# Projection by 512 tokens for eleven column groups, gelu and forget columns copied by ScalarE, row maxima paced by due steps, first attention operands loaded during the projection

## The chip, the cores and the metric

The kernel runs on one core of one Trainium2 chip. A core has TensorE (PE in the profile; PEld is its weight load), VectorE (DVE), ScalarE (ACT), GpSimd (POOL) and SyncE (SP), which here issues every DMA. The metric is the device time of one execution in microseconds; a comparison takes the median of several runs of each kernel.

## What is computed

One layer of a decoder trunk over 4096 tokens of width 1024, all in float32. The input is normed and projected to 3848 columns; three mixers read them, and their 1024 output columns are projected back, added to the input and normed.

```
h = rmsnorm(x, norm_g);  proj = h @ w_in          # (4096, 1024) @ (1024, 3848)
a_u a_v a_z | b_q b_fl b_i b_z | c_q c_k c_v c_z c_fl = split(proj)   # 256 each, c_*: 512, c_fl: 8
y_a = gelu(a_u) * (tril(w_s) @ layernorm(gelu(a_v)) + b_s) * silu(a_z)   # per 128-token chunk and group of 64
y_b = hgrn2(b_q, b_fl, b_i) * silu(b_z)           # gated linear recurrence, chunks of 128, 4 heads
y_c = softmax(c_q c_k^T / 8 + cumulative log-forget, causal) c_v * silu(c_z)   # 8 heads of 64
out = rmsnorm(x + [y_a | y_b | y_c] @ w_out, final_norm_g)
```

## The kernel before

Products of float32 matrices are split: an operand is held as a high part (type fp32r) and the rest (low part), and a product is the sum of high x high, high x low and low x high. So a projection over 1024 input rows is a chain of 8 x 3 = 24 matmuls into one PSUM buffer.

**Projection phase** (L177 to L1088). The tokens form 16 tiles of 256 (T), in 4 blocks of BT = 4. The loop at L1037 takes for each block the 15 column groups in the list `order` (b_fl, b_q, b_i, c_k, c_q, c_v, c_z, a_v, a_u, a_z, b_z; the last block has its own order, with c_v at the end), and for each group the four tiles: 60 steps to a block, 240 in all. A step calls `project` (L891): two halves, each of 24 matmuls with a moving operand of 256 columns, into one buffer acc of 2 x 256. In feature-major groups (c_q, c_k, c_z, b_fl, b_q; L902) the weights are stationary and 256 tokens move; in the others (L923) 128 tokens are stationary and 256 weight columns move, so the output has tokens on the partitions. b_i also carries the 8 forget columns of C (264 columns). There are two acc buffers (psa), so a step waits until the result of the step before the last has been copied out by `evac` (L841).

The order on TensorE is the program's order, written out by hand (manual_schedule); the other engines' order and the buffers of each pool are set by a scheduler. Between steps the loop advances a set of generators by one yield each, so that their TensorE work stands between projections: `xprep` (L256: load, norm, transpose the input of a tile, split it into hhi and hlo, in hT), `hgrn` (L413: the recurrence of one tile, 7 levels that each take a decay tile e from POOL, L493 and L494), `gm_v`, `gm_u`, `gm_z` (L753 to L814, the gMLP branch, whose gelu at L741 first copies acc with VectorE, L744), `hg_z`, `cgen` (the cumulated log-forget), and in the last block `prerm` (L948), the row maxima of the first U0 = 3 attention units. y_a and y_b are made with tokens on the partitions and turned by four transposes in `y_store` (L791, L797). Weights for the next group are loaded in a group's first step and split in the next two (L227, L228). Four tiles of hT exist; tile T is given up after its step of the last group, b_z (L1054), and the next block's input takes its place.

**Attention phase** (from L1092). A unit u = (p, Q) is a pair of heads p (4) with 512 queries Q (8): 32 units. Unit u goes over groups j = 0..Q of 512 keys, 144 groups in all; a group has 8 score tiles (`do_tile`, L1372: two matmuls, L1380 and L1383, then the exponential on ScalarE, L1387), indexed n = 0..7, two to a step si. The weighted values (`do_pv`, L1280) of a group are taken in the next group at n = 2, and `do_accs` (L1263) sums the probabilities on VectorE and POOL. When a unit is done, `finish_unit` sums its denominators (pl, L1223) and divides.

The softmax needs each row's maximum before the scores. A generator `rowmax` (L1145) makes them ahead: a step of it is two products (L127) into a buffer sm of which there are two, reduced by VectorE (L140, or L135 on the diagonal); after a unit's last product `rm_tail` (L1173) waits 6 yields, transposes the maxima through the same two buffers (mt, L1181) and copies them (L1183). Pacing: a step at n = 0, 1, 4, 6 of each group always, and at n = 3, 5, 7 while the count of maxima is below 2 * si + LEAD, LEAD = 8 * NJ + 12 = 76. A unit takes 8 * (Q + 1) maxima. Ahead of each unit's load, steps are forced until its maxima are there (L1429). Keys come into 26 buffers (big); a list `need` with due steps orders their loads, and unit 0's qa and qc are loaded at the start of the phase (L1361).

**Output phase** (from L1442): for each 128 tokens two chains of 24 matmuls with 512 columns (L1481), the residual and the final norm.

Of the kernel before, what the change touches and what calls it, by code (L numbers as in the profile page):

```python
# [33 lines left out]
def tile_trunk(  # L34
# [27 lines left out]
    const = ctx.enter_context(tc.tile_pool(name="const", bufs=1))  # L62
    dram = ctx.enter_context(tc.tile_pool(name="dram", bufs=1, space=DRAM))
# [46 lines left out]
    def load_keys(t, p, j):  # L110

        nc.sync.dma_start(t[0:64].bitcast(F32), prow(d_kh[j], p))
        nc.sync.dma_start(t[64:68].bitcast(F32), d_cb[j][2 * p : 2 * p + 2].rearrange("h r t -> r h t"))

# [62 lines left out]
    with ExitStack() as p1:  # L177
        cst = p1.enter_context(tc.tile_pool(name="cst", bufs=1))
        hp = p1.enter_context(tc.tile_pool(name="hp", bufs=BT))
        wp = p1.enter_context(tc.tile_pool(name="wp", bufs=2))  # L180
        xp = p1.enter_context(tc.tile_pool(name="xp", bufs=4))
# [60 lines left out]
        def x_ssq(t, ss):  # L242
            junk = wk.tile([P, D], BF16, tag="junk", name="junk")
            nc.scalar.activation(junk, t, AF.Square, accum_out=ss)
# [11 lines left out]
        def xprep(T, own_norm=False):  # L256

            xts = [x_load(2 * T + half) for half in range(2)]
# [14 lines left out]
            while len(hT) >= BT:  # L273
                yield
            hi = hp.tile([P, KC, 256], F32R, tag="hhi", name="hhi")
            lo = hp.tile([P, KC, 256], F32R, tag="hlo", name="hlo")
            hT[T] = (hi, lo)
            for half in range(2):
# [8 lines left out]
                for kk in range(2):  # L287
                    dst = (slice(None), slice(4 * kk, 4 * kk + 4), slice(half * P, half * P + P))
# [12 lines left out]
        def setup_gen():  # L301

            setup["lng"] = row_bcast("lng", ln_g.rearrange("o g c -> o (g c)"), 256)
            off = setup["off"] = row_bcast("lnb", ln_b.rearrange("o g c -> o (g c)"), 256)
# [8 lines left out]
            ws = wk.tile([P, 4, P], F32, tag="e", name="ws", bufs=3)  # L313
# [18 lines left out]
            nc.tensor.transpose(pt2[:, 4:6], lbr, ident[:2, :2])  # L332
            nc.vector.tensor_copy(bsT, pt2[:, 0:4])

# [24 lines left out]
            nc.vector.tensor_tensor(off4, off4, bcast(bsT[:, :, None], [P, 4, 64]), op=ALU.add)  # L359

# [7 lines left out]
            for li, h in enumerate(levels[2:]):  # L368
                nblk = 64 // h
                mt = wk.tile([P, 64], F32, tag="e", name="mt", bufs=3)  # L370
# [12 lines left out]
                m16 = wk.tile([P, 16], F32, tag="e", name="m16", bufs=3)  # L383
# [29 lines left out]
        def hgrn(T):  # L413
# [5 lines left out]
            l = wk.tile([P, 512], F32, tag="e", name="l", bufs=3)  # L419
# [20 lines left out]
            qk = wk.tile([P, 512], F32, tag="e", name="qk", bufs=3)  # L440
# [5 lines left out]
            for st in range(len(levels) + 4):  # L446
# [1096 lines left out]
```

## Time and profile before

| what | us |
|---|---|
| runs: median of three (lowest to highest) | 3445.62 (3445.28 to 3450.19) |
| profiled execution | 3452.37 |
| its span, first to last instruction | 3450.7 |
| TensorE busy in the span | 3316.0 |
| VectorE busy | 2367.5 |
| ScalarE busy | 1614.1 |
| GpSimd busy | 1428.7 |

The profile is of one execution; its span starts with the first instruction. A row of the costliest groups names line, engine, operation, output and inputs, shape and count, then the busy time of the group, the mean ns of one, and the idle time of the engine just ahead of them with what ended it. Weight loads, matmuls and DMAs have rows of their own. fp32 matmuls that are not split appear as two records each.

### The profile page before, as it was taken

The page shows a single profiled execution, that of the slowest core. Times are in us where ns is not written, and L with a number is a line of the kernel's source. Part 1 is how long each engine was busy: PE and PEld are TensorE (multiplying, and loading weights), DVE is VectorE, ACT ScalarE, POOL GpSimd, SP SyncE. Part 2 cuts the span into 40 slices and gives each one's busy share as a digit, 9 for nine tenths or more (in the row PEclk, how much of TensorE's full clock was granted, in tenths as well). Part 3 has the DMA queues.
Part 4 walks back from the last instruction along what each step waited for, and adds up shares of the span by engine and source line. Part 5 has one row for each costly group of instructions (what it writes and reads, how often), then busy time and mean ns, then how long its engine had stood idle before and what let it go on. Part 6 is the DMA issues. An engine that isn't in the chain of part 4 may idle for free.

```text
span 3450.7 us, 62925 instructions
## 1 busy us (share of the span) xinstructions
PE 3316.0 (96%) x24375; PEld 2634.7 (76%) x24375; DVE 2367.5 (69%) x4551; ACT 1614.1 (47%) x2947; POOL 1428.7 (41%) x1504
## 2 busy tenths in 40 slices
PE   7999999999999999989899999999999999999998
PEld 7999999999999999889555555555555555548887
DVE  6467745586457855695488788888888888755554
ACT  6335553356434453354255455555555555552221
POOL 2134422243224431343266566666666666660000
PEclk9999999999999999999799999999999999999999
DMA  5332243214232133211641142014201311014442
GB/s 181 112 96 66 77 138 118 84 53 156 90 109 75 41 112 115 73 53 56 156 113 27 30 120 67 24 34 124 66 24 34 108 50 42 28 65 147 144 144 98
DMA packets 227596, 297.70 MB, mean 86 GB/s; under 512 B 19602, under 2 KB 172448, under 8 KB 227298
## 3 DMA queue, kind: packets, MB, share of 16 engines
q1 hardware_dynamic: 227298, 293.69, 28.1%
q8 instruction: 191, 3.13, 0.4%
q14 instruction: 107, 0.88, 0.1%
HBM read 208.96 MB, written 84.43 MB: 85 GB/s over the span
## 4 chain that ended last, share of the span: by engine, by line
PE 72%; DVE 18%; ACT 3%; DMA 2%; POOL 2%; issue 2%; SPq 0%; DVEq 0%; POOLq 0%; ACTq 0%
PE acc L902 16%; PE pv L1280 12%; PE acc L923 11%; PE o L1481 10%; PE st L1380 7%; PE sm L127 6%; PE st L1383 6%; DVE mp L140 3%; DVE acc L1263 3%; DVE wlo L228 2%; DMA x<-in_x_dram 2%; PE pl L1223 1%; DVE gt L746 1%; DVE xq L511 1%; PE plb L574 1%
## 5 line engine op out<-in xcount | busy, mean ns | idle before, releaser
L1387 ACT ACTIVATE pt<-st,bias 128x512 f32<-128x512 f32 (+3 forms) x1152 | 700.4, 651 | 499.0 <-PE st L1383 466.9
L1263 POOL TENSOR_TENSOR acc<-acc,pt 128x512 f32<-128x512 f32 (+2 forms) x516 | 639.0, 1238 | 303.1 <-PE st L1380 221.3
L140 DVE TENSOR_REDUCE mp<-sm 128x2 f32<-128x1024 f32 (+1 forms) x460 | 535.4, 1191 | 163.6 <-PE sm L127 163.1
L902 PE MATMUL acc<-hhi,whi 128*128 128x256 f32 x2048 | 580.0, 288 | 4.2 <-DVE q L735 2.6
L902 PE MATMUL acc<-hhi,wlo 128*128 128x256 f32 x2048 | 568.0, 282 | 0.0
L902 PE MATMUL acc<-hlo,whi 128*128 128x256 f32 x2048 | 567.4, 281 | 0.1
L923 PE MATMUL acc<-whi,hhi 128*128 128x256 f32 (+1 forms) x1792 | 518.0, 289 | 18.5 <-DVE gu L744 16.1
L923 PE MATMUL acc<-wlo,hhi 128*128 128x256 f32 (+1 forms) x1792 | 507.0, 283 | 0.0
L923 PE MATMUL acc<-whi,hlo 128*128 128x256 f32 (+1 forms) x1792 | 506.8, 283 | 0.0
L1280 PE MATMUL pv<-pt,v 128*64 128x512 f32 (+3 forms) x2304 | 503.7, 578 | 0.8 <-POOL pt L1392 0.6
L1380 PE MATMUL st<-qa,ka 128*128 128x512 f32 (+2 forms) x1152 | 466.9, 407 | 18.0 <-DMA ka<-d_kl 12.5
L1263 DVE TENSOR_TENSOR acc<-acc,pt 128x512 f32<-128x512 f32 (+2 forms) x516 | 414.4, 803 | 91.7 <-PE pv L1280 51.7
L1383 PE MATMUL st<-qc,kb 68*128 68x512 f32 (+2 forms) x1152 | 442.9, 385 | 1.4 <-DMA qc<-mr 0.8
L127 PE MATMUL sm<-kb,qb 66*128 66x512 f32 (+2 forms) x1152 | 359.2, 394 | 33.2 <-DVE mp L140 26.0
L902 PEld LDWEIGHTS acc<-hhi,whi 128*128 128x128 f32 x2048 | 384.5, 190 | 7.9 <-DVE q L735 3.0
L902 PEld LDWEIGHTS acc<-hhi,wlo 128*128 128x128 f32 x2048 | 384.4, 190 | 0.0
L902 PEld LDWEIGHTS acc<-hlo,whi 128*128 128x128 f32 x2048 | 383.9, 189 | 0.5 <-DVE hlo L290 0.3
L1280 PEld LDWEIGHTS pv<-pt,v 128*64 128x64 f32 x2304 | 158.0, 140 | 286.5 <-issue 265.0
L1380 PEld LDWEIGHTS st<-qa,ka 128*128 128x128 f32 x1152 | 220.7, 192 | 185.8 <-issue 126.1
L923 PEld LDWEIGHTS acc<-whi,hhi 128*128 128x128 f32 x1792 | 341.8, 191 | 22.3 <-DVE gu L744 16.6
L923 PEld LDWEIGHTS acc<-wlo,hhi 128*128 128x128 f32 x1792 | 342.1, 191 | 0.1
L923 PEld LDWEIGHTS acc<-whi,hlo 128*128 128x128 f32 x1792 | 341.5, 191 | 0.0
(265 smaller groups left out, 5131.9 us busy)
## 6 DMA issues: line engine op xcount, KB each, us to landing
wraw<-in_w_in_dram SPq DMA_DIRECT2D x120, 512.0 KB
x<-in_x_dram SPq DMA_DIRECT2D x88, 512.0 KB
qa<-d_qh SPq DMA_DIRECT2D x64, 256.0 KB
out_dram<-x SPq DMA_DIRECT2D x31, 512.0 KB
kb<-d_kh SPq DMA_DIRECT2D x38, 256.0 KB
d_kh<-chi SPq DMA_DIRECT2D x32, 256.0 KB
d_kl<-clo SPq DMA_DIRECT2D x32, 256.0 KB
d_qh<-chi SPq DMA_DIRECT2D x32, 256.0 KB
```

Source lines behind the costliest of these rows:

```text
L127: nc.tensor.matmul(ps[:, :n], qb[0:66, h, i * P : (i + 1) * P], kb[0:66, h, :n], start=True, stop=True)
L140: nc.vector.tensor_reduce(dst, ps, axis=AX.X, op=ALU.max)
L228: nc.vector.scalar_tensor_tensor(lo[:, k, :n], raw, g, hi[:, k, :n].bitcast(F32), op0=ALU.mult, op1=ALU.subtract)
L511: nc.vector.tensor_tensor(xq[rows, :, r, :].rearrange("p g (n h) -> p g n h", h=h), sl(e), sl(qf), op=ALU.mult,)
L902: nc.tensor.matmul(ps[:, a, :], ww[:, k, cs], hh[:, k, :], start=n == 0, stop=n == 3 * KC - 1)
L923: nc.tensor.matmul(o, hh[:, k, ts_], ww[:, k, :width], start=n == 0, stop=n == 3 * KC - 1)
L1263: ins = eng.tensor_tensor(a[:, q0:], src[:, q0:], pts[i][:, q0:], op=ALU.add)
L1280: mm = nc.tensor.matmul(pv[64 * h : 64 * h + 64, q0:], vt[:, i, 64 * h : 64 * h + 64], group[h][i][:, q0:], start=kb == 0, stop=kb == nkb - 1,
L1380: first = nc.tensor.matmul(st[:, qm:], ka_t[g][:, h, cs], qa_t[u % 2][:, h, qm:], start=True, stop=False)
L1383: nc.tensor.matmul(st[:, qm:], kb_t[g][0:68, h, cs], qc_t[u % 2][:, h, qm:], start=False, stop=True)
L1387: nc.scalar.activation(pt[:, q0:], st[:, q0:], AF.Exp, bias=bias_of[u][:, h, kb : kb + 1])
L1481: nc.tensor.matmul(ps, a[:, k % 4, o : o + P], b[k][:, cs], start=n == 0, stop=n == 3 * KC - 1)
```

## The change

- Hidden tiles hold 512 tokens (J = T // 2), two of them in place of four; a pair is given up after two steps of b_z. Eleven groups (b_fl after the first block's, b_q, c_k, c_q, c_z, and now also a_u, a_z, b_z) are projected with 128 stationary weight columns and 512 moving tokens (`project_fm`); a step is one half a of the columns for 512 tokens instead of both halves for 256. Only b_i, c_v0, c_v1 and a_v keep tokens on the partitions.
- The gMLP branch and the gate of B work with features on the partitions: the mixing product is transposed, its affine part is one fused VectorE operation for each half, y_a needs no transposes, and y_b's gate is applied as the transposed tile is read.
- gelu's first copy goes from VectorE to ScalarE; the forget columns are copied by ScalarE, and GpSimd adds their bias.
- Buffers: xp is kept for all phases; tag e has 2 in place of 3, st 4 in place of 5, f and q 3 of double size in place of 5 and 4; the attention's big has 24 in place of 26.
- `prerm` may start from the third group of the last block; after it, `preload` loads unit 0's qa, qc, ka and kb into the xp buffers.
- Row maxima: steps at n = 3, 5, 7 are taken while the count is below `rm_due`; the tail waits 5 yields and is advanced right after a product instead of ahead of the next; no step at n = 0, 1 of the first group. A unit's closing work is advanced at n = 5, 6, 7 in place of 4, 5, 7. LEAD, which now only orders key loads, is 88.

```diff
-        hp = p1.enter_context(tc.tile_pool(name="hp", bufs=BT))
+        hp = p1.enter_context(tc.tile_pool(name="hp", bufs=BT // 2))
...
-            while len(hT) >= BT:
+            while J not in hT and len(hT) >= BT // 2:
                 yield
-            hi = hp.tile([P, KC, 256], F32R, tag="hhi", name="hhi")
-            lo = hp.tile([P, KC, 256], F32R, tag="hlo", name="hlo")
-            hT[T] = (hi, lo)
+            if J not in hT:
+                hT[J] = tuple(hp.tile([P, KC, 512], F32R, tag=f"h{c}", name=f"h{c}") for c in ("hi", "lo"))
+            hi, lo = hT[J]
...
-                    e = wk.tile([P, 512], F32, tag="e", name="e", bufs=3)
+                    e = wk.tile([P, 512], F32, tag="e", name="e", bufs=2)
...
-            nc.vector.tensor_copy(dst, ps)
+            nc.scalar.copy(dst, ps)
             nc.scalar.activation(t, dst, AF.Square)
...
+            pm = pst.tile([P, 2, 256], F32, tag="tp", name="pm")
+            gv = g.rearrange("p (c n) -> p c n", c=2)
+            for a in range(2):
+                for c in range(2):
+                    for r in (1, 0):
+                        gi = 2 * a + r
+                        nc.tensor.matmul(
+                            pm[64 * r : 64 * r + 64, a, c * P : c * P + P], gv[:, c, gi * 64 : gi * 64 + 64],
+                            setup["wT"][:, gi, :], start=True, stop=True,
+                        )
...
+        def gm_z(J, a, ps):
+            t = wk.tile([P, 512], F32, tag="st", name="gz", bufs=4)
+            silu(ps, t)
+            yield
+            nc.gpsimd.tensor_tensor(t, t, Mx[J][:, a, :], op=ALU.mult)
...
+        token_major = {"b_i", "c_v0", "c_v1", "a_v"}
+
+        def project_fm(J, a, whi, wlo):
+            hi, lo = hT[J]
+            ps = psa.tile([P, 512], F32, tag="acc", name="acc")
+            cs = slice(a * P, a * P + P)
+            n = 0
+            for k in range(KC):
+                for ww, hh in ((whi, hi), (whi, lo), (wlo, hi)):
+                    nc.tensor.matmul(ps, ww[:, k, cs], hh[:, k, :], start=n == 0, stop=n == 3 * KC - 1)
+                    n += 1
+            return ps
...
+                    fl = FL[:, 2 * T + a, :]
+                    nc.scalar.copy(fl, ps1[:, 256:264])
+                    nc.gpsimd.tensor_tensor(fl, fl, setup["bf"], op=ALU.add)
...
+                wide = gi > 0 and g not in token_major
+                J, a = (T // 2, ti % 2) if wide else (T // 2, None)
+                while not (({2 * J, 2 * J + 1} if wide else {T}) <= h_done):
                     x_tick()
+                ps = project_fm(J, a, hi, lo) if wide else project(g, T, hi, lo, first=gi == 0)
+                if gi % len(order) == len(order) - 1 and ti % 2 == 1:
+                    hT.pop(J)
...
+        def preload():
+            for _ in range(4):
+                yield
+            for k, rows in (("qa", P), ("kb", P), ("ka", P), ("qc", 68)):
+                first_ops[k] = xp.tile([rows, 2, 512], F32R, tag="x", name=f"{k}0")
...
+            load_q(0, 0, first_ops["qa"], first_ops["qc"])
+            load_keys(first_ops["kb"], 0, 0)
+            yield
+            load_m(first_ops["qc"], d_m[0])
+            load_k_hilo(first_ops["ka"], 0, 0)
...
-        big = p2.enter_context(tc.tile_pool(name="big", bufs=26))
+        big = p2.enter_context(tc.tile_pool(name="big", bufs=24))
...
                         rm_pair(ps, qb, kb_t[p * NJ + cj], hi_, cj == Q, tri, mp, cj)
+                        tick(tails)
                         yield
...
-            for _ in range(2 if u == 0 else 6):
+            for _ in range(2 if u == 0 else 5):
...
-        NSLOT, NV, LEAD = 26, 10, 8 * NJ + 12
+        NSLOT, NV, LEAD = 24, 10, 8 * NJ + 24
...
+        due = [(first_step[u] - 4, 2 * first_step[u] + 8 * (Q + 1) + 16) for u, (p, Q) in enumerate(units) if u >= U0]
+
+        def rm_due(si):
+            return max([n - 2.5 * max(d - si, 0) for d, n in due if d >= si - 8], default=0)
...
-                if n in (0, 1, 4, 6):
+                if n in (0, 1, 4, 6) and (gi or n > 3 or not U0):
                     rm_step()
-                if n in (3, 5, 7) and rm_count[0] < 2 * si + LEAD:
+                if n in (3, 5, 7) and rm_count[0] < rm_due(si):
                     rm_step()
...
-                if n in (4, 5, 7):
+                if n in (5, 6, 7):
                     tick(fin)
```

More of the change, by code (lines that the diff above doesn't have):

```diff
@@ L359, in setup_gen @@
             nc.vector.tensor_tensor(off4, off4, bcast(bsT[:, :, None], [P, 4, 64]), op=ALU.add)
+            po_ = pst.tile([P, 2, P], F32, tag="tp", name="offp")
+            for a in range(2):
+                nc.tensor.transpose(po_[:, a, :], off[:, a * P : a * P + P], ident)
+            nc.vector.tensor_copy(offT, po_)
             lm = cst.tile([P, 5, 16], U8, name="lm")
@@ L634, in hgrn @@
             yield
-            sq = wk.tile([P, 512], F32, tag="e", name="sq", bufs=3)
+            sq = wk.tile([P, 512], F32, tag="e", name="sq", bufs=2)
             pof = po.rearrange("p a b v -> p (a b) v")
@@ L861, in evac @@
                 for dst, src in ((dh, hi), (dl, lo)):
-                    nc.sync.dma_start(
-                        dst[J][half * 256 : half * 256 + 256, o : o + 256].rearrange("(a p) t -> p a t", p=P),
-                        src.bitcast(F32),
-                    )
-            elif g[:3] == "c_v":
+                    nc.sync.dma_start(dst[J][rows, :], src.bitcast(F32))
+            elif g[:3] == "c_z":
+                zt = wk.tile([P, 512], F32, tag="st", name="cz", bufs=4)
+                silu(ps, zt)
+                nc.sync.dma_start(d_z[J][rows, :], zt)
+            elif g == "b_z":
+                if J not in Hz:
+                    Hz[J] = wk.tile([P, 2, 512], F32, tag="q", name="hz", bufs=3)
+                silu(ps, Hz[J][:, a, :])
+                if a == 1:
+                    for T in (2 * J, 2 * J + 1):
+                        spawn(hg_y(T))
+            elif g == "a_u":
+                spawn(gm_u(J, a, ps))
+            elif g == "a_z":
+                spawn(gm_z(J, a, ps))
+        def evac(g, T, ps):
+            J, o = T // 2, (T % 2) * 256
+            if g[:3] == "c_v":
                 half = int(g[3])
-                vt = wk.tile([P, 2, 256], F32, tag="st", name="cv", bufs=5)
+                vt = wk.tile([P, 2, 256], F32, tag="st", name="cv", bufs=4)
                 nc.vector.tensor_copy(vt, ps)
@@ L948, in prerm @@
         def prerm():
-            tri = wk.tile([P, 512], F32, tag="junk", name="tri0")
+            tri = wk.tile([P, 2, 512], F32, tag="f", name="tri0", bufs=3)[:, 0, :]
             make_tri(tri)
@@ L980, in prerm_tail @@
             yield
-            mr = wk.tile([16, P], F32R, tag="st", name="mr0", bufs=5)
+            mr = wk.tile([16, P], F32R, tag="st", name="mr0", bufs=4)
             nc.vector.tensor_copy(mr, pt)
@@ L1074, in tile_trunk @@
                 tick(cq)
-                if ps is not None:
+                if wide:
+                    evac_fm(g, J, a, ps)
+                elif g not in token_major:
+                    evac_fm(g, J, None, flat(ps), T % 2)
+                elif ps is not None:
                     evac(g, T, ps)
@@ L1166, in rowmax @@
                 yield
-                for t in list(tails):
-                    try:
-                        next(t)
-                    except StopIteration:
-                        tails.remove(t)
+                tick(tails)
         def rm_tail(u, mp):
@@ L1325, in load_next @@
             _, kind, i = need.popleft()
-            slots[0] -= 1
+            slots[0] -= i not in apart
             if kind:
```

245 lines of the change are left out of this document (125 added, 120 removed).

## The prediction, made before the change was run

> **What bounds the kernel now.** I read the page first: engine shares, the chain of work that ended last, the costliest groups.
>
> ```profile
> span 3450.7 us, 62925 instructions
> ...
> PE 3316.0 (96%) x24375; PEld 2634.7 (76%) x24375; DVE 2367.5 (69%) x4551; ACT 1614.1 (47%) x2947; POOL 1428.7 (41%) x1504
> ...
> PE 72%; DVE 18%; ACT 3%; DMA 2%; POOL 2%; issue 2%; SPq 0%; DVEq 0%; POOLq 0%; ACTq 0%
> ...
> L902 PE MATMUL acc<-hhi,whi 128*128 128x256 f32 x2048 | 580.0, 288 | 4.2 <-DVE q L735 2.6
> ...
> L923 PE MATMUL acc<-whi,hhi 128*128 128x256 f32 (+1 forms) x1792 | 518.0, 289 | 18.5 <-DVE gu L744 16.1
> ```
>
> TensorE carries 72% of the chain and VectorE 18%. The two groups are one third each of the projection: 3 x (2048 + 1792) = 11,520 matmuls of 256 columns, 48 to a step. Their mean of 288 ns is no price, since matmuls overlap in the records; the price is the spacing of their starts, which the chain in order of time gives for unbroken runs.
>
> ```profile
> 506.68 11.37 PE acc L902 x96
> ...
> 1641.03 22.74 PE acc L923 x192
> ...
> 3093.60 348.40 PE o L1481 x1536
> ```
>
> 22.74 us / 192 = 118.4 ns per matmul of 256 columns, 11.37 / 96 the same; the output stage's 512 columns cost 348.40 / 1536 = 226.8 ns. Then I cut the span into stages, for busy time and granted clock (columns: window, its length, busy PE, PEld, DVE, ACT, POOL, PEclk, DMA share, GB/s).
>
> ```profile
> 340.00:360.00 20.00, 14.60 (x151) 14.16 (x149) 19.27 (x60) 10.54 (x21) 6.13 (x6) 1.00 0.16 43
> 434.00:834.00 400.00, 392.13 (x4217) 384.99 (x4217) 251.91 (x561) 191.32 (x373) 127.73 (x125) 0.99 0.31 98
> 1236.00:1664.00 428.00, 405.99 (x4244) 395.13 (x4242) 262.00 (x608) 176.33 (x345) 130.71 (x131) 0.97 0.25 76
> 1664.00:1697.00 33.00, 18.65 (x48) 12.65 (x50) 14.84 (x15) 6.24 (x11) 8.12 (x19) 0.56 1.00 212
> 1950.00:1990.00 40.00, 36.37 (x138) 21.01 (x138) 30.51 (x60) 16.55 (x30) 21.03 (x26) 0.83 0.23 64
> ```
>
> A middle block of the projection (434 to 834) has PE busy 98%, VectorE 63%. So time taken off TensorE there counts, except where VectorE is full: 340 to 360, the a_v steps, where it is busy 96%. The hand-over at 1664 is the worst stretch: PE busy 57% at a clock of 0.56.
>
> **The change part by part.** The sum is made against the profiled execution, 3452.37 us (span 3450.7 and 1.7 around it). It stands 6.7 us above the median of the runs, 3445.62.
>
> *Projection by 512.* Still at 256 columns: b_i, c_v0, c_v1, a_v (4 x 16 steps x 48 = 3072) and b_fl of the first block (192). The other 8256 become 4128 of 512. Each saves 2 x 118.4 - 226.8 = 10.0 ns: 41.3 us, all on the bounding engine. The nearest other rows with 512 columns are the attention's scores:
>
> ```profile
> 3051.66 0.40 PE L1380 MATMUL st<-qa,ka 128*128 128x512 f32 x1
> ...
> 3052.36 0.39 PE L1383 MATMUL st<-qc,kb 68*128 68x512 f32 x1
> ```
>
> Three starts in 0.70 us are 233 ns, which would save 3.5 ns a pair, 14 us. I take 41: the output stage has the same unbroken sums of 24 products of 128 x 128 weights; ends 14 and 41. The Trainium skill (TensorE: Matmul & The Clock Gate, "Back-to-back issue gap") puts the isolated spacing at N/2.4 + 2.5 ns, which gives 2.5 ns saved a pair, 10 us; the two rows above contradict it with 118.4 and 226.8.
>
> *gMLP, features first.* The a output no longer needs its transposes, and the mixing product becomes 16 records with 64 weight columns instead of 8 with 128.
>
> ```profile
> 383.42 1.06 PE L774 MATMUL pm<-gv,wT 128*128 128x128 f32 x8
> 384.24 0.36 PE L923 MATMUL acc<-whi,hhi 128*128 128x256 f32 x1
> ...
> 810.58 0.60 PE L797 MATMUL ytp<-ident,gz 128*128 128x128 f32 x4
> 810.93 0.36 PE L923 MATMUL acc<-whi,hhi 128*128 128x256 f32 x1
> ...
> L603 PE MATMUL po<-v,sc 128*64 128x64 f32 x512 | 17.7, 222 | 0.0
> ```
>
> Four transposes delay the next matmul by 0.35 us: 16 tiles, -5.6. The mixing product now takes 384.24 - 383.42 = 0.82 us; L603, with 64 weight columns, gives 17.7 / 512 = 35 ns a record at half as many columns, so 16 records take 0.6 to 1.6 us. I take 1.0: +3 (-4 to +13). VectorE trades its 682 ns class of copies for as many fused passes; POOL loses two products a tile and is not on the path.
>
> *gelu's copy on ScalarE.* In each of the first three blocks TensorE waits for the copy that frees its PSUM buffer:
>
> ```profile
> 360.40 0.58 PE L923 MATMUL acc<-whi,hhi 128*128 128x256 f32 x1 [5.32 <-DVE gu L744]
> L744 DVE COPY gv<-acc 128x512 f32<-128x512 f32 x16 | 10.9, 682 | 0.0
> L1217 ACT COPY rt<-pv 128x512 f32<-128x512 f32 x32 | 18.6, 583 | 54.5 <-PE pv L1280 54.5
> ```
>
> 16.1 us in all (the group above), each wait followed by a few us at reduced clock. The copy was late because VectorE was full at 340 to 360, where ScalarE is busy 53%. There it costs about 583 ns instead of 682 and stands behind little. VectorE sheds 4 x 0.68 = 2.7 us before this point, so its backlog halves but is not gone, and what comes next (the mixing product waits for VectorE's rsqrt chain) keeps some of the wait. I take -15, clock included, between 0 and -25. The forget column's copy (8 columns) is the same kind and priced at nothing: ScalarE has half its time free there; uncovered, its 32 pieces cost at most 0.58 us each, 19.
>
> *Hidden tiles in pairs.* A 512-token tile comes free only after two steps of b_z, so the next block's second pair is prepared late: the last half tile is transposed right ahead of the third step of b_fl, which needs it.
>
> ```profile
> L289 ACT CAST hhi<-xtp 128x512 fp32r<-128x512 f32 x64 | 33.9, 589 | 27.6 <-PE xtp L284 27.6
> L290 DVE TENSOR_TENSOR hlo<-xtp,hhi 128x512 fp32r<-128x512 f32 x64 | 40.5, 680 | 1.4 <-ACT hhi L289 1.0
> ```
>
> TensorE then waits for one cast and one subtraction, 0.59 + 0.68 = 1.3 us, three times: 4; behind queued weight splits up to 5 each. I take +6 (+3 to +15). SP's queue holds the x loads one step longer; what is queued behind them, the stores, has that slack.
>
> *The hand-over.* The first attention operands are loaded during the projection.
>
> ```profile
> 1663.78 0.59 SPq L1138 DMA_DIRECT2D qa<-d_qh  x1
> ...
> 1676.27 0.77 PE L1380 MATMUL st<-qa,ka 128*128 128x512 f32 x1 [12.52 <-DMA ka<-d_kl]
> 1677.66 0.58 SPq L1138 DMA_DIRECT2D qa<-d_qh  x1
> 1679.02 1.19 PE L127 MATMUL sm<-kb,qb 66*128 66x512 f32 x2 [1.56 <-DMA qb<-d_qh]
> ```
>
> 12.5 us of idling, then 20 us at half clock (0.56 over the window): 22 us lost. Afterwards the first eight score tiles start at once, but the row maxima's qb and unit 1's qa are still issued after the projection's end: about 6 and 11 issues of 0.59 us, 3.6 and 6.5 us, with a few us to land. TensorE has some 4 us of work for that, so 5 to 6 us of waiting in two pieces and part of the slow clock remain: half the loss. -12 (-5 to -20).
>
> *Row maxima by due steps.* I walked the loop by hand. Before, the lead of 76 is reached in five groups and then held; unit 7 has 64 maxima and its tail needs 7 more steps, so four steps are forced in a row ahead of it. After, one extra step a group raises the lead to 88 by unit 7, and nothing is forced.
>
> ```profile
> 1958.33 1.19 PE L127 MATMUL sm<-kb,qb 66*128 66x512 f32 x4
> 1960.88 0.93 PE L127 MATMUL sm<-kb,qb 66*128 66x512 f32 x2 [1.36 <-DVE mp L140]
> ...
> 1993.41 0.27 PE L1181 MATMUL mt<-ident,m 128*16 128x128 f32 x1
> 1994.52 0.73 PE L127 MATMUL sm<-kb,qb 66*128 66x512 f32 x2 [0.83 <-DVE mp L140]
> L1181 PE MATMUL mt<-ident,m 128*16 128x128 f32 x29 | 8.2, 282 | 0.2 <-DVE mp L140 0.2
> L127 PE MATMUL sm<-kb,qb 66*128 66x512 f32 (+2 forms) x1152 | 359.2, 394 | 33.2 <-DVE mp L140 26.0
> L1223 PE MATMUL pl<-acc,ones_v 128*64 128x512 f32 x128 | 51.5, 618 | 6.5 <-DVE acc L1263 4.2 <-ACT rt L1217 2.4
> ```
>
> The burst costs its wait of 1.4 us and a clock of 0.83 over 40 us (6.8): -7 (-3 to -9). The same walk puts every transposed row (mt) right before a product one tile behind the last one (24 times a wait near 0.83, 20 us; all such waits sum to 26.0); after the change it stands between products two tiles apart, which leaves about half: -10 (0 to -20). Sums one tile later: of pl's 6.5 us, -3 (0 to -5).
>
> Priced at nothing: the first-block row maxima shifted by six steps onto the a_v steps of the last block (cover: TensorE idles 22 of 428 us there already; +-8), and two attention buffers fewer at the end (+-5).
>
> Sum: -41.3 - 5.6 + 3 - 15 + 6 - 12 - 7 - 10 - 3 = -85. 3452.4 - 85 = 3367 for a profiled execution, 3361 against the median.
>
> **The rivals.** *VectorE takes the place of TensorE* (0.20): the copies leave it, but fused gates and wide affine passes come, while its steps shorten. Then the a_v wait returns behind the rsqrt chain (+15), the last block loses 8, the boundaries 9 more: -53, 3393. For it the 96% of 340 to 360; against it the 63% of the block.
>
> *Little from width* (0.05): the pairs save what the score rows say, 14 instead of 41: -58, 3388. The skill's rule above belongs here; by it the sum is -54.
>
> *Everything clears* (0.12): the a_u wait and its clock go whole (-25), the hand-over -20, the mt waits -18, no boundary cost: about -123, 3323.
>
> *Slower* (0.05): the decay tiles (tag e) fall from three buffers to two, so POOL's write of the next level waits until VectorE has read the one before.
>
> ```profile
> POOL e L493 <- DVE xl L505: 80.5, 15, 11.1
> L493 POOL TENSOR_TENSOR e<-z 128x256 f32<-128x256 f32 x112 | 81.7, 730 | 274.6 <-PE pla L543 117.0 <-DVE xl L505 80.5 <-DVE oss L640 53.6
> ```
>
> Such waits are there already, 80.5 us, none on the path. There are 112 levels, each fed by two such POOL passes (1.5 us); if TensorE came to wait over 0.76 us per level, the 85 us are gone; at 1.1 us it is +38, 3484. Against it: one level a step of over 6 us, and 1.5 us of POOL in it.
>
> **How the numbers follow.** The forecast has 0.58. Its terms' ends, which will not all fall to one side, give about +-32: 3329 to 3393. The VectorE and width rivals end inside or near that; up to 3408 takes their spread in, and 3325 is as far as the clearing case needs; outside lie its better half and the slower case, below 0.2. A measurement of this kernel can tell about 0.2%, 7 us, from no change. Faster 0.94, within 0.2% 0.02, slower 0.04 (the buffer case alone, of which a part ends level).
>
> **What would show it.** 4128 matmuls of 128x512 in the projection with 226.8 ns between starts (233 would refute the first term); no idle behind a gelu copy at a_u; a wait of 1 to 5 us ahead of the third b_fl step in blocks 1 to 3; the first score matmul within 2 us of the projection's end; no run of four row-maximum pairs; idle before them well under 33 us. The prediction is wrong if the middle blocks do not shorten from 400 to about 383 us, or if the attention stretch grows.

## The result and the profile after

The changed kernel takes 3429.13 us, the median of four runs (3425.58 to 3431.68); the kernel before, run beside it, 3447.9 (3445.28 to 3454.14). The ratio is 0.994 with an interval of 0.9923 to 0.9957: 19 us, 0.6%, faster. The forecast was 85 us, to 3361 us, in a range of 3329 to 3393. The profiled execution after took 3426.99 us, its span 25.4 us less than before; that is more than the 19 us of the medians, since the profiled execution before was one of the longer ones (3452.37) and that after one of the shorter.

The page of the changed kernel: busy time, then three groups that answer to those of before (projection, score product, row maxima).

```profile
PE 3282.2 (96%) x20314; PEld 2414.1 (70%) x20314; DVE 2341.9 (68%) x4521; ACT 1615.3 (47%) x2979; POOL 1386.3 (40%) x1504
...
L952 PE MATMUL acc<-hhi,whi 128*128 128x512 f32 x1376 | 557.6, 405 | 13.6 <-ACT gu L777 11.0
...
L1474 PE MATMUL st<-qa,ka 128*128 128x512 f32 (+2 forms) x1152 | 470.8, 411 | 22.2 <-DMA qa<-d_qh 16.1
...
L149 PE MATMUL sm<-kb,qb 66*128 66x512 f32 (+2 forms) x1152 | 359.1, 394 | 20.0 <-DVE mp L162 12.2
```

The work is there as designed: 3 x 1376 = 4128 wide matmuls, idle ahead of the row maxima down from 33.2 to 20.0 us. But the wait for gelu's copy is still there, now on ScalarE, and the score product has waits of 16.1 us for its queries that were not there before.

The chain in order of time, for the spacing of starts:

```profile
1583.27 11.14 PE acc L952 x48
...
1597.70 5.55 PE acc L952 x24
...
3068.58 348.40 PE o L1575 x1536
```

11.14 us / 48 = 232 ns and 5.55 / 24 = 231 ns for a wide matmul of the projection; the output stage is where it was, 226.8.

Stages of the changed kernel: the a_v steps and a middle block, then the first 300 us and the rest of the attention phase; below them the same two stretches before.

```profile
340.00:360.00 20.00, 18.71 (x170) 15.91 (x170) 17.41 (x47) 10.49 (x20) 7.63 (x6) 1.00 0.00 1
437.00:833.00 396.00, 387.69 (x3186) 329.12 (x3185) 245.90 (x554) 190.51 (x382) 116.86 (x126) 0.99 0.32 100
...
1651.00:1951.00 300.00, 267.90 (x1072) 158.42 (x1072) 222.06 (x297) 136.47 (x225) 155.22 (x175) 0.86 0.33 78
1951.00:3068.00 1117.00, 1090.41 (x4801) 628.25 (x4797) 915.25 (x1313) 636.43 (x1062) 744.69 (x787) 0.99 0.23 61
```

```profile
1676.00:1976.00 300.00, 288.50 (x1197) 168.90 (x1197) 238.67 (x349) 149.16 (x251) 169.78 (x193) 0.92 0.34 80
1976.00:3093.00 1117.00, 1080.67 (x4674) 613.51 (x4673) 895.23 (x1258) 617.46 (x1036) 729.10 (x764) 0.99 0.22 61
```

Three readings. A middle block takes 396 us where 383 was forecast. From the first score matmul to the first of the output stage it is 1417.3 us in both kernels, so the attention phase gained nothing. (The profiles of e_halves, e_stride, e_stridefm, e_gelu and e_fl, which leave this phase as it is, have 1411.6 to 1416.9: a few us in a stage are no effect.) But that nought is two changes: in its first 300 us the changed kernel gets through 1072 matmuls against 1197, at a clock of 0.86 against 0.92, and then through more in the rest (4801 against 4674).

So the 25.4 us of the span came from two places: the hand-over (first score matmul 1.06 us after the last projection matmul, before 12.8, from start to start), and the projection, 1649.4 to 1635.9 us. The second is at its upper end: in e_pace, e_pace88, e_tail8 and e_ycpool, which leave the projection as the changed kernel has it, it took 1638.8 to 1641.6 us, so 8 to 13 us were gained there.

### The profile page after: what moved, and what is told of

The parts are those of the page before. It is cut to its first block, busy times and chain, and to the rows that moved or that the text cites. A ratio compares the mean times of both kernels' runs of the same rounds, so it can differ in the third digit from the quotient of the medians.

```text
span 3425.3 us, 54796 instructions
## 1 busy us (share of the span) xinstructions
PE 3282.2 (96%) x20314; PEld 2414.1 (70%) x20314; DVE 2341.9 (68%) x4521; ACT 1615.3 (47%) x2979; POOL 1386.3 (40%) x1504
## 4 chain that ended last, share of the span: by engine, by line
PE 52%; DVE 10%; POOL 2%; issue 1%; ACT 1%; DMA 1%; SPq 0%; DVEq 0%; POOLq 0%; ACTq 0%
PE pv L1367 12%; PE o L1575 10%; PE st L1474 7%; PE acc L952 7%; PE sm L149 6%; PE st L1477 6%; DVE mp L162 3%; DVE acc L1350 3%; PE acc L988 2%; POOL acc L1350 1%; PE pl L1310 1%; DVE wlo L249 1%; DMA qc<-d_ql 0%; DVE rn L1317 0%; DVE sm L157 0%
## 5 line engine op out<-in xcount | busy, mean ns | idle before, releaser
L952 PE MATMUL acc<-hhi,whi 128*128 128x512 f32 x1376 | 557.6, 405 | 13.6 <-ACT gu L777 11.0
L952 PE MATMUL acc<-hlo,whi 128*128 128x512 f32 x1376 | 544.8, 396 | 1.3 <-DVE hlo L313 1.3
L952 PE MATMUL acc<-hhi,wlo 128*128 128x512 f32 x1376 | 545.4, 396 | 0.0
L1474 PE MATMUL st<-qa,ka 128*128 128x512 f32 (+2 forms) x1152 | 470.8, 411 | 22.2 <-DMA qa<-d_qh 16.1
L249 DVE SCALAR_TENSOR_TENSOR wlo<-wraw,gT,whi 128x256 fp32r<-128x256 f32 (+1 forms) x480 | 255.6, 572 | 76.6 <-ACT whi L248 75.3
L952 PEld LDWEIGHTS acc<-hhi,wlo 128*128 128x128 f32 x1376 | 259.8, 189 | 60.8
L988 PE MATMUL acc<-whi,hhi 128*128 128x256 f32 (+1 forms) x1024 | 295.3, 288 | 7.6 <-ACT FL L995 5.7
L988 PE MATMUL acc<-wlo,hhi 128*128 128x256 f32 (+1 forms) x1024 | 289.3, 283 | 0.0
L988 PE MATMUL acc<-whi,hlo 128*128 128x256 f32 (+1 forms) x1024 | 289.2, 282 | 0.0
L149 PEld LDWEIGHTS sm<-kb,qb 66*128 66x128 f32 x1152 | 217.4, 195 | 80.8 <-DVE mp L162 26.3
L1477 PEld LDWEIGHTS st<-qc,kb 68*128 68x128 f32 x1152 | 224.8, 195 | 36.4 <-DMA qc<-d_m 1.0
```

The lines of the kernel that those rows point to most:

```text
L149: nc.tensor.matmul(ps[:, :n], qb[0:66, h, i * P : (i + 1) * P], kb[0:66, h, :n], start=True, stop=True)
L249: nc.vector.scalar_tensor_tensor(lo[:, k, :n], raw, g, hi[:, k, :n].bitcast(F32), op0=ALU.mult, op1=ALU.subtract)
L952: nc.tensor.matmul(ps, ww[:, k, cs], hh[:, k, :], start=n == 0, stop=n == 3 * KC - 1)
L988: nc.tensor.matmul(o, hh[:, k, ts_], ww[:, k, :width], start=n == 0, stop=n == 3 * KC - 1)
L1474: first = nc.tensor.matmul(st[:, qm:], ka_t[g][:, h, cs], qa_t[u % 2][:, h, qm:], start=True, stop=False)
L1477: nc.tensor.matmul(st[:, qm:], kb_t[g][0:68, h, cs], qc_t[u % 2][:, h, qm:], start=False, stop=True)
```

## The experiments

Theory from the two traces: (1) a wide matmul saves about 5 ns a pair, not 10; (2) the even pace of the row maxima costs the start of attention some 30 us; (3) unit 2's operands are late because a store stands ahead of them; (4) the forget copy on ScalarE holds TensorE at b_i. Rivals stand with each run. All edits are made to the changed kernel except in e_beforefm. Times are medians of four to nine runs, and differences without a further word are against the changed kernel's 3429.1. The kernel before, run beside each of them, had medians of 3448.1 to 3451.0 against 3447.9 here, so such a difference is good to some 3 us. Sums over spacings, times per group and sums of idle and half-clock time are worked out from the starts and the granted clock in the records.

### e_halves: the width undone

```diff
-                    nc.tensor.matmul(ps, ww[:, k, cs], hh[:, k, :], start=n == 0, stop=n == 3 * KC - 1)
+            for c in range(2):
+                hs = slice(256 * c, 256 * c + 256)
...
+                        nc.tensor.matmul(
+                            ps[:, hs], ww[:, k, cs], hh[:, k, hs], start=n == 0, stop=n == 3 * KC - 1
+                        )
```

> The changed kernel, with each 512-token chain of the projection made as two chains of 256 tokens into the two halves of the same bank; everything else stays. Theory (a wide matmul saves about 6 ns over two narrow ones, 232 against 2 x 118.4 ns, in 4128 pairs): 20 to 28 us longer, 3449 to 3457. Rival one (the prediction's, 226.8 against 236.8): 41 us longer, 3470. Rival two (the stretches beside the matmuls take what the width gives, since chains end less often): under 10 us longer, 3439 or less.

Measured: 3441.74 us, +12.6; the projection 1651.1 against 1635.9. Between theory and the second rival. Averaged over the records that follow each other unbroken, a narrow matmul stands 118.4 ns from the next and a wide one 231.8: 2 x 118.4 - 231.8 = 5.0 ns a pair, 4128 pairs, 20.6 us. The 12.6 measured are less; that the waits for other engines take back the rest is likely and not shown.

### e_stride and e_stridefm: where the 5 ns come from

In 40 unbroken chains of the changed kernel the spacing depends on the place in the chain alone (235.0 ns at the third place, 237.6 at the thirteenth, 225.8 at the nineteenth, each with a standard deviation under 1 ns), whatever the other engines do. That points to addresses. The split weights lie at 264 columns a row block because one group needs 264. Here they are packed at their own number of columns n, in e_stride for all groups, in e_stridefm for the eleven feature-major ones (fm); the edit is that of e_stridefm.

```diff
                 pair = tuple(wp.tile([P, KC, 264], F32R, tag=f"w{c}", name=f"w{c}") for c in ("hi", "lo"))
+                if fm:
+                    pair = tuple(
+                        t.rearrange("p k c -> p (k c)")[:, : KC * n].rearrange("p (k c) -> p k c", c=n) for t in pair
+                    )
```

> The changed kernel, with the split weights of the 256-column groups packed at 256 columns a row block instead of 264 (the tile keeps its size, and the group with the forget columns its 264). The starts of the projection's 512-token matmuls follow one fixed pattern in every chain, 226 to 238 ns by the place in the chain (mean 231.5, deviation 0.4 at each place), whatever the other engines do; the output stage's go at 226.7. Theory (the pattern comes from where the weights lie): the spacing falls to 227, 5 ns less in 4128 wide matmuls and in up to 2304 narrow ones: 20 to 32 us shorter, 3397 to 3409. Rival (it comes from something else, the instruction stream or the tokens' tiles): within 4 us of the changed kernel, and the pattern stays.

> The changed kernel, with the weights packed at 256 columns a row block for the eleven feature-major groups alone; the token-major groups keep 264. With all groups packed, the 512-token matmuls went from 231.8 to 227.8 ns (226.8 in the unbroken chains) and the token-major ones of 256 columns from 118.2 to 119.9, and the time fell by 8 us. Theory (stationary weights read at a step of 1024 bytes load without the extra 5 ns, weights as the moving operand lose by it): 12 to 16 us below the changed kernel, 3413 to 3417. Rival (the token-major loss was the stalls', not the step's): 3419 to 3423 as with all groups packed.

Measured: e_stride 3421.19 us, -7.9, and e_stridefm 3413.76, -15.4. The chain of e_stridefm over the steps shown above:

```profile
1579.68 10.93 PE acc L956 x48
...
1593.90 5.49 PE acc L956 x24
```

10.93 / 48 = 227.7 ns; in 40 unbroken chains every spacing from the third place on is now 226.6 to 226.9 (mean 226.8), the output stage's pace. The theory holds. With all groups packed, the token-major matmuls of 256 columns, where the weights are the moving operand, went from 118.2 to 119.9 ns, 4 us over 2304 of them; leaving those at 264 keeps that loss away. (In the two profiles the projection takes the same, 1632 us; the 7 us between the two medians are not seen there.) The extra 5 ns are set by where the stationary operand's row blocks lie, at a step of 1056 or of 1024 bytes; whether by the step itself or by the addresses that come of it, and why, no run shows.

### e_beforefm: the same packing in the kernel before

> The kernel before the change, unchanged but for the weights of the feature-major groups packed at 256 columns a row block in place of 264. Theory (the 5 ns above the pace of the columns are one cost a matmul, set by where its stationary weights lie, so the narrow matmuls carry it twice a pair; the prediction read the output stage's 226.8 ns as what any 512-column matmul takes): the narrow feature-major matmuls fall from 118.3 to about 113.4 ns, 8256 of them, so up to 40 us in unbroken pace, less what the waits for the other engines take back; 3410 to 3425 us, below the changed kernel's 3429 without any wide matmul. Rival (narrow matmuls are held by something of their own at 118 ns, and packing helps wide ones alone): 3444 to 3454.

Measured: 3456.94 us against 3448.07, ratio 1.0027 (1.0017 to 1.0037): slower, by 0.3%. The theory fell, the rival holds for narrow matmuls. Of the 8256 matmuls that the expectation counts, 6144 are feature-major in this kernel; the other 2304 belong to a_u, a_z and b_z, where the packed weights are the moving operand. Starts within one feature-major chain in time order:

```profile
148.95 0.28 PE L906 MATMUL acc<-hhi,wlo 128*128 128x256 f32 x1
...
150.15 0.28 PE L906 MATMUL acc<-hhi,whi 128*128 128x256 f32 x1
```

Ten steps in 1.20 us: 120 ns. Over all unbroken feature-major records it is 119.9 where the kernel before has 118.4, so a narrow matmul loses 1.5 ns by the packing. It is held at 118 to 120 by something else, and the gain of width depends on the layout: 5.0 ns a pair as it was written, 2 x 118.4 - 226.8 = 10.0 when the weights are packed. The prediction's price was that of a layout that this kernel does not have.

### e_gelu: gelu's copy back on VectorE

```diff
-            nc.scalar.copy(dst, ps)
+            nc.vector.tensor_copy(dst, ps)
```

> The changed kernel, with gelu's copy out of the bank again on VectorE. Theory (the copy on ScalarE shortened the wait at the group of the u columns, 5.5 us in three blocks before the change and 3.2 + 0.9 us after it, about 1.4 us a block): 2 to 8 us longer, 3431 to 3437. Rival one (the prediction's, the whole wait hung on VectorE: up to 5 us a block): 10 to 20 us longer, 3439 to 3449. Rival two (ScalarE's own queue is the longer one, and the copy is better on VectorE): 3425 or less.

Measured: 3435.03 us, +5.9, inside the theory's range. The effect is small, and the intervals of the two ratios overlap (0.9948 to 0.9973, the changed kernel's 0.9923 to 0.9957); the waits show it more surely. What TensorE waited for in the projection (us in all, times, longest), e_gelu first, then the changed kernel, then the kernel before:

```profile
PE acc L952 <- DVE gu L777: 19.7, 6, 5.7
...
PE acc L988 <- ACT FL L995: 5.9, 4, 1.8
```

```profile
PE acc L952 <- ACT gu L777: 11.0, 6, 3.0
PE pm L811 <- DVE mp L157: 8.1, 1, 8.1
PE acc L988 <- ACT FL L995: 5.7, 4, 1.8
```

```profile
PE acc L923 <- DVE gu L744: 16.1, 3, 5.4
```

With the copy on VectorE and everything else as changed, the wait would be 19.7, more than the 16.1 before; the move to ScalarE takes 8.7 of it, and 11.0 stay, now for a copy that is late on ScalarE.

### e_fl: the forget columns back on VectorE

```diff
-                    nc.scalar.copy(fl, ps1[:, 256:264])
-                    nc.gpsimd.tensor_tensor(fl, fl, setup["bf"], op=ALU.add)
+                    nc.vector.tensor_tensor(fl, ps1[:, 256:264], setup["bf"], op=ALU.add)
```

> The changed kernel, with the eight forget columns again added on VectorE straight from the bank, in place of ScalarE's copy and GpSimd's add. Theory (the copy behind ScalarE's other work holds the bank, and costs TensorE about 2.8 us a block at the token-major group): 8 to 12 us shorter, 3417 to 3421, and the wait of that group for ScalarE's forget copy is gone. Rival (VectorE is as late there, or the next bank's wait takes its place): within 4 us of 3429.

Measured: 3431.14 us, no difference.

```profile
PE acc L952 <- ACT gu L777: 10.9, 6, 3.0
PE acc L988 <- DVE FL L995: 9.5, 9, 1.6
```

The wait stays, and is longer (9.5 against 5.7), so the copy's engine is not its cause; theory (4) fell. Both copies out of that PSUM buffer come late. ScalarE's queue at the wait in the second block of the changed kernel:

```profile
487.56 1.04 ACT L265 ACTIVATE junk<-x 128x1024 bf16<-128x1024 f32 x1
...
488.60 0.70 ACT L770 ACTIVATE t<-t,ones_c 128x512 f32<-128x512 f32 x1
489.21 0.35 ACT L993 COPY v<-acc 128x256 f32<-128x256 f32 x1
```

The first 256 columns are copied behind a square of the input norm and passes of a gate, and the forget columns behind them. Which edit put those there was not separated. Both kernels copy the 256 columns on ScalarE.

### e_late: the operands loaded after the projection

`preload` no longer runs beside the last projection steps; the attention phase begins with it, into the same buffers.

```diff
-                if pre_on and not pre and len(pre_on) == 1:
-                    pre.append(preload())
-                    pre_on.append(True)
...
         if U0:
+            for _ in preload():
+                pass
             qa_t, qc_t = [first_ops["qa"]] + qa_t, [first_ops["qc"]] + qc_t
```

> The changed kernel, with the loads of the first attention operands issued only after the projection's last matmul, into the same buffers. Theory (the early loads are what took away the gap of 12.8 us between the last projection matmul and the first score matmul; 1.06 us is left in the changed kernel): the gap is back at 5 to 13 us, with a stretch of half clock behind it, 7 to 15 us longer, 3436 to 3444, and the rest of the attention part as in the changed kernel. Rival (the loads of unit 1 and its keys, behind these in SyncE's queue, then take the place of the wait: the gap was only moved): within 5 us of 3429.

Measured: 3426.64 us, no difference, and the gap stays at 1.06 us. The forecast missed, and not for the rival's reason: the edit did not make the loads late. SyncE's queue, e_late, then the kernel before with what SyncE waited for there (us in all, times, longest):

```profile
1469.99 0.58 SPq L119 DMA_DIRECT2D qa<-d_qh  x1
```

```profile
1663.78 0.59 SPq L1138 DMA_DIRECT2D qa<-d_qh  x1
...
SPq L1138 <- PE acc L923: 4.5, 1, 4.5
```

SyncE runs ahead of TensorE: though the load now stands behind the projection in the program, it is still issued at 1470, 183 us before the projection's last matmul. In the kernel before, the same load stood 4.5 us in SyncE's queue until the projection's last matmul was done. So what makes the loads early is that their buffers belong to a pool of their own (xp), and no longer to memory that the projection holds to its end, and not their place in the program. That early loads take away the gap fits both traces; this run, whose loads are early too, does not test it.

### e_pace, e_pace88, e_tail8: the pace of the row maxima

Undo the even pace; replace it by the old kind with a larger constant; keep it and transpose later.

```diff
-                if n in (3, 5, 7) and rm_count[0] < rm_due(si):
+                if n in (3, 5, 7) and rm_count[0] < 2 * si + 8 * NJ + 12:
...
-                if n in (3, 5, 7) and rm_count[0] < rm_due(si):
+                if n in (3, 5, 7) and rm_count[0] < 2 * si + LEAD:
...
-            for _ in range(2 if u == 0 else 5):
+            for _ in range(2 if u == 0 else 8):
```

These are the edits of e_pace (8 * NJ + 12 is 76), e_pace88 (LEAD is 88) and e_tail8, each made alone.

> The changed kernel, with only the pace of the row maxima as before the change: a step at the odd places whenever the lead is under 76, in place of the even schedule. Theory (the even pace costs the start of attention): with five steps in 21 of the first 27 groups, the transpose of the row maxima waits for VectorE and the half clock follows each such wait; the trace of the changed kernel falls 36 us behind by group 28. Without it the first 28 groups should come 20 to 30 us earlier, and the burst of forced steps at group 27 (about 5 us) and part of what is regained later go lost again: 3404 to 3419 us, 10 to 25 below the changed kernel. Rival one (the pace is harmless, the loss lies in the transposes standing later in the group and in the late operands of units 1 and 2): within 5 us of the changed kernel's 3429. Rival two (the even pace does pay over the whole attention part): 3434 or more.

> The changed kernel, with the old kind of pace (a step at every odd place while the lead is under a constant) but the constant at 88 in place of 76; by the walk seven full groups of seven steps come first, no step is forced later, and the transpose falls on the fifth place of the group in the steady part, as in the changed kernel. Theory (the even pace costs about 30 us in the first 28 groups, and the steady gain of 0.2 us a group hangs on the place of the transpose, not on the pace): 3400 to 3412 us, behind the kernel before by under 15 us at group 28 and 9.3 us a group afterwards. Rival (the row maxima are a fixed amount of VectorE's work, and wherever they are done the whole attention part takes its 1417 us): 3425 to 3434.

> The changed kernel, with the transpose of a unit's row maxima three steps later (eight steps behind the unit's last pair in place of five); by the walk of the plan it then falls on the second place of a group in nearly every unit, where the kernel before had it, and not on the fifth. Theory (the place in the group is worth 0.2 us a group: 9.31 us a group in groups 40 to 100 of the changed kernel, 9.52 in the kernel before and in the run with the old pace, which both have it on the second place): 15 to 22 us lost in the steady part, some 9 us of waits at the transpose and their half clock saved in the first 27 groups; 3435 to 3445 us, and about 9.5 us a group. Rival (the place does not matter, the steady gain comes from elsewhere): 3415 to 3432, and 9.3 us a group.

Measured: e_pace 3430.62 us (no difference: a miss), e_pace88 3400.01 (-29.1), e_tail8 3412.19 (-16.9: a miss to the other side). By its time alone e_pace would speak against theory (2). The stages of e_pace, then of e_pace88, then of e_tail8:

```profile
1654.00:1954.00 300.00, 280.05 (x1171) 163.88 (x1172) 235.37 (x337) 148.62 (x249) 168.84 (x198) 0.93 0.34 80
1954.00:3071.00 1117.00, 1083.26 (x4698) 614.73 (x4697) 898.66 (x1273) 621.56 (x1038) 720.46 (x764) 0.98 0.22 61
```

```profile
1654.00:1954.00 300.00, 280.96 (x1177) 163.66 (x1178) 237.13 (x347) 149.06 (x249) 167.84 (x191) 0.93 0.34 79
1954.00:3043.00 1089.00, 1065.49 (x4692) 613.76 (x4691) 894.57 (x1262) 623.17 (x1039) 728.77 (x771) 0.99 0.22 62
```

```profile
1657.00:1957.00 300.00, 269.62 (x1138) 159.10 (x1138) 234.00 (x328) 145.22 (x242) 165.10 (x184) 0.92 0.34 79
```

With either constant the first 300 us are nearly as fast as before the change (1171 and 1177 matmuls against 1197, clock 0.93). The phase in two parts, with what of each part TensorE idled and what the half clock took (the time times the share of the clock that was not granted), in us:

| run | first 28 groups | idle, half clock | from there on | idle, half clock |
|---|---|---|---|---|
| before | 291.8 | 11.2, 19.6 | 1125.4 | 36.3, 18.8 |
| changed | 328.2 | 34.8, 44.4 | 1089.1 | 23.6, 6.8 |
| e_pace | 297.7 | 19.8, 21.3 | 1119.8 | 33.7, 26.5 |
| e_pace88 | 299.0 | 19.0, 22.2 | 1090.7 | 23.5, 8.5 |
| e_tail8 | 307.3 | 31.1, 23.9 | 1089.9 | 26.3, 8.5 |

So the changed kernel loses 36 us in 28 groups and gets as much back behind them. e_pace wins the first and loses the second: 29 us against e_pace88, 18 of them half clock and 10 idle. Groups 40 to 100 take 9.52 us each in e_pace and 9.53 in the kernel before, 9.3 in the other three. The transpose's place in the group does not decide that: e_tail8 has it on the second place like e_pace, and takes 9.29. What does stays open.

What the even pace does to the start, by what TensorE waited for in these 300 us, the changed kernel, then e_tail8, then e_pace88:

```profile
PE st L1474 <- DMA qa<-d_qh: 16.1, 2, 10.6
PE mt L1272 <- DVE mp L162: 8.9, 4, 3.2
```

```profile
PE st L1474 <- DMA qa<-d_qh: 15.8, 2, 10.3
...
PE mt L1272 <- DVE mp L162: 1.4, 3, 0.5
```

```profile
PE st L1474 <- DMA qa<-d_qh: 6.6, 2, 3.4
```

With five steps to a group and sums besides, VectorE is behind, and a transpose five yields after the last product finds its maxima unfinished: here VectorE's queue at the wait of 3.2 us, four sums ahead of the reductions.

```profile
1763.68 2.35 DVE L162 TENSOR_REDUCE mp<-sm 128x2 f32<-128x1024 f32 x2
1765.95 4.88 DVE L1350 TENSOR_TENSOR acc<-acc,pt 128x512 f32<-128x512 f32 x4
1770.75 2.34 DVE L162 TENSOR_REDUCE mp<-sm 128x2 f32<-128x1024 f32 x2
```

Each such wait is paid a second time by the clock. The wait of 1.72 us in the changed kernel, and the stretches behind it (PEclk is the third number from the end):

```profile
1725.96 0.33 PE L1272 MATMUL mt<-ident,m 128*16 128x128 f32 x1 [1.72 <-DVE mp L162]
...
1726.00:1736.00 10.00, 10.00 (x27) 6.56 (x29) 5.57 (x6) 3.80 (x6) 3.39 (x5) 0.50 0.45 104
1737.00:1747.00 10.00, 10.00 (x53) 6.25 (x50) 8.66 (x10) 4.97 (x9) 4.97 (x11) 1.00 0.40 95
```

Half clock for 10 us, 27 matmuls instead of 53. The four waits of the changed kernel, 8.9 us, came with stretches of 10.2, 13.7, 10.2 and 10.2 us at half clock, which is up to 22 us more. In e_tail8 these waits are down to 1.4 us, the clock is back at 0.92, and the attention phase falls from 1417.3 to 1397.2 us; in e_pace88 the wait for unit 2's queries is short too, and it falls to 1389.7. So theory (2) holds, with the transposes as the larger part of it. What costs is the even pace and a tail of five yields together; the even pace with the old tail of six was not run.

### e_ycpool: the store on GpSimd

In the changed kernel SyncE's queue stands still before unit 2's loads:

```profile
1678.75 0.26 SPq L115 DMA_DIRECT2D kb<-d_cb  x1
1693.53 0.34 SPq L1323 DMA_DIRECT2D d_yc<-rt  x1
...
1695.88 0.58 SPq L119 DMA_DIRECT2D qa<-d_qh  x1
```

```diff
-            nc.sync.dma_start(d_yc[p][Q], t)
+            nc.gpsimd.dma_start(d_yc[p][Q], t)
```

> The changed kernel, with the store of a finished unit's values issued by GpSimd, which makes them, in place of SyncE. Theory (in SyncE's queue the store waits for GpSimd's product, 13.5 us at unit 0, and the loads of unit 2 stand behind it, so TensorE waits 10.6 us for them): that wait is gone, with its half clock 10 to 16 us, 3413 to 3419 us. Rival one (the loads are late for another reason, or the time is made up behind it since VectorE is what is short there): within 4 us of 3429. Rival two (the issues on GpSimd delay its sums and with them the tiles of exponentials): 3434 or more.

Measured: 3467.4 us, +38.3: rival two, and by more than it said. Over the attention phase of e_ycpool, with the changed kernel's rows behind:

```profile
PE pl L1310 <- DVE acc L1350: 11.9, 4, 4.4
...
PE st L1474 <- DMA qa<-d_qh: 9.5, 2, 5.0
PE st L1474 <- ACT pt L1481: 6.7, 6, 4.7
```

```profile
PE st L1474 <- DMA qa<-d_qh: 16.1, 2, 10.6
...
PE st L1474 <- ACT pt L1481: 5.4, 6, 3.4
PE pl L1310 <- DVE acc L1350: 4.7, 4, 2.0
```

The wait for the queries does shrink (16.1 to 9.5), so (3) was right about the queue; but others grow, and the phase's mean clock falls from 0.96 to 0.95. The attention phase takes 1454.2 us against 1417.3, 36.9 more: idle time is 8 of them, half clock 26 (77 us against 51); behind the first 28 groups it is 37.5 against 6.8. The issues themselves are short (0.58 us each, 32 of them, on GpSimd); how they bring about these waits was not followed further.

### e_best: three edits together

The pace of 88, the packed feature-major weights, and unit 0's last product and store one place later, so that unit 2's loads stand ahead of them.

```diff
             yield
+            if u == 0:
+                yield
             nc.gpsimd.tensor_tensor(t, t, r, op=ALU.mult)
             nc.sync.dma_start(d_yc[p][Q], t)
```

> The changed kernel with three edits: the constant pace of 88 for the row maxima (29 us below the changed kernel by itself), the feature-major weights packed at 256 columns (15 us below by itself), and the last product and the store of unit 0 one place later, so that the loads of unit 2 go ahead of that store in SyncE's queue. Theory (the three lie in different stretches and add up, and the wait for unit 2's operands, 3.2 us with the constant pace, goes too): 3378 to 3390 us, a wait under 1 us at unit 2's first score matmul. Rival one (they add up, but the store takes its wait elsewhere): 3384 to 3394 with the wait still there. Rival two (the shorter projection is eaten by its waits for the other engines once the rest moves): 3395 to 3402.

Measured: 3381.98 us (3381.81 to 3386.57), ratio to the kernel before 0.9808 (0.9795 to 0.9822): 47 us below the changed kernel, 68 below the one before, at the sum of the parts (29.1 + 15.4 = 44.5) and a little more. In its first 300 us:

```profile
PE st L1480 <- DMA qa<-d_qh: 3.3, 1, 3.3
```

One wait, that of unit 1; unit 2's, 3.2 us in e_pace88, is gone, and the attention phase falls from 1389.7 there to 1380.1. A reordering within SyncE's queue removed that wait without the cost of moving the store to another engine.

## Why the prediction was wrong

The direction was right and the size was not: -85 forecast, -25.4 in the profiled executions. Four terms carry the difference of 60.

- **Projection by 512, -41.3: measured -20.6 in pace** (e_halves: 12.6 of the whole). The failing step is "I take 41: the output stage has the same unbroken sums of 24 products of 128 x 128 weights". The sums are the same, the place of the weights is not. The nearer row was the other one, the score products' 233 ns. By an estimate from the spacing that the Trainium skill gives (TensorE: Matmul & The Clock Gate, "Back-to-back issue gap") a pair would have saved 2.5 ns; the runs show 5.0, and 10.0 packed.
- **Row maxima by due steps, -7 - 10 - 3: measured 0.** The single effects were there (no burst, idle ahead of the products 33.2 to 20.0), and from the 29th group on the phase is 36 us shorter. The step that failed counted what the old walk costs and nothing for the new one: an extra step in 21 of the first 27 groups, on an engine that has 4.88 us of sums in a group, with a tail one yield shorter, 36 us longer by the 28th. e_pace88 against the changed kernel: 27.6 us of attention.
- **gelu's copy, -15: measured -5.9.** "Its backlog halves but is not gone" was said, and yet nearly the whole wait of 16.1 us was priced. It went to 11.0 us.
- **Nothing was priced at b_i**, where the forget column's copy stood at nothing for "ScalarE has half its time free there". The share was an average: the chains of b_i took 94.3 us before and 105.3 after, by the spacing of their starts; 7 us of it is idle time and 3 half clock. That it comes from the copy's engine is refuted by e_fl; which edit makes both copies late stays open.

Of the other terms, the mixing product cost +3.3 for +3 (0.81 to 1.02 us, 16 tiles). The pairs of hidden tiles cost 1.3 us at each of three boundaries ahead of the third b_fl step, as worked out (+3.8 for +6). The row maxima of the first units, moved by 27 us, met the mixing product and the recurrence (8.1 and 5.1 us of waits) and relieved other waits of that block: inside the +-8.

The hand-over looks right and is so in part by luck. Its -12 was a net figure, with 5 to 6 us of waiting and part of the slow clock left. The gap alone fell by 11.7; "unit 1's qa" then waits 5.4 us as forecast, and unit 2's, which was not thought of, 10.6. The net can be read from e_pace, which does as many row-maximum steps in its first five groups (33) as the kernel before: its sixth group starts 75.1 us after the projection's last matmul, before 81.4. That is a gain of 6.3, inside the range and half of the forecast.

Of the rivals, "Little from width" had the nearer figure for the first term, 14 where 20.6 was measured; why the score products stand 233 ns apart no run shows. "VectorE takes the place of TensorE" named the right engine at the wrong place: in a middle block it is busy 62% (245.90 of 396), and the time was lost to its queue in the attention phase.

## What to carry to other kernels

A price taken from another stage holds only if the operands lie the same way: compare the spacing of starts by place in the chain, and try the layout by itself before the shape. When work is spread evenly over a busy engine, ask what waits in order behind it, and count a short wait of TensorE at more than its length: waits of about 2 us cost 2 to 7 us here, with the half clock behind them. A queue that runs ahead is freed by buffers, not by an earlier place in the program.

## What the runs showed of the hardware

- A wide matmul's pace depends on where its stationary weights lie: 231.5 ns on average at row blocks of 1056 bytes, with a fixed pattern of 226 to 238 by place; 226.8 from the third place on at 1024. A narrow matmul does not gain (118.4 and 119.9).
- A wait of TensorE of 1.72 us was followed by 10 us at half clock. The Trainium skill (TensorE: Matmul & The Clock Gate, "HAM oscillation — how this bites in real kernels") gives the rule that no idle gap should exceed about 3.4 us; here a gap of half that was enough. It is not always: waits of 1.3 to 2.4 us in the attention phase were followed by 3.4 to 13.7 us at half clock in most cases (3.4 after 1.68 in the kernel before), and by none after 1.96 us in e_best.
- Stores issued by GpSimd in place of SyncE cost 38 us in 32 issues of 0.58 us; 26 us of it is time at half clock.
